# A two-layer diffusion step on one core: the low parts of layer 0's projection weights move from GpSimd to VectorE

## The chip, the core and the metric

The kernel runs on one core of one Trainium2 chip. The metric is device time in microseconds, the median of several runs. TensorE (PE) multiplies matrices, VectorE (DVE), ScalarE (ACT) and GpSimd (POOL) compute elementwise, and SyncE (SP) and GpSimd issue the DMAs. Each engine works through its own queue of instructions in the order in which the program lists them.

## The reference, cut to what matters

One inference step of a backbone with two layers, width 1024, for 512 latent tokens and 128 context tokens, in float32. Layer 0 projects the modulated input once, and splits the product between neighbourhood attention and RWKV-7 heads:

```python
proj = h @ w_in                                    # 1024 -> 3*512 + 1792
qa, ka, va, u = jnp.split(proj, [D_NA, 2 * D_NA, 3 * D_NA], axis=-1)
...
o_na = na_latent(qa, ka, va, na_ctx[0], na_ctx[1], rpb)   # softmax_attn_blocked for context tokens
o_rw, S_fin = rwkv_mixer(u, S0, *rw)                      # two directions, state scans
y = jnp.concatenate([o_na, o_rw], axis=-1) @ w_out
```

Then come a gated channel mixer (SwiGLU), layer 1 with differential attention and its mixer, and a final norm.

## The kernel before

Activations lie transposed: 128 features on the partitions, 640 tokens along the free dimension (512 latent, 128 context), in two halves of 320. Every large product is made of three: a float32 weight w is split into a rounded high part wh and the rest wl = w - wh, the input likewise into hh and hl, and TensorE adds wh x hh, wh x hl and wl x hh. `load_w` (L336) fetches a weight tile and splits it:

```python
        SY.dma_start(raw[:, 0:n], src)                                        # wr, L341
        ...
        A.copy(wh[:, 0:n], raw[:, 0:n])                                       # wh on ScalarE, L344
        eng = (V, G)[lo_turn[0] % 2] if cur.get("alt") else cur["lo"]         # L345
        lo_turn[0] += 1
        eng.tensor_tensor(wl[:, 0:n], raw[:, 0:n], wh[:, 0:n], ALU.subtract)  # wl, L347
```

Layer 0 has 26 projections of 128 output columns; each takes two such tiles of 128 x 512 (raw tiles: 3 buffers; wh and wl: 3 each) and 48 matmuls into PSUM tiles named `pj` (in the profile, all matmuls have line L99, that of the helper). The first four are computed ahead; `proj_units` (L1037) lists the rest: a gate, then for head pairs 1 to 3 the RWKV inputs k, r and v (`kkrv_proj`: ScalarE copies us, L966 to L971; VectorE shifts tokens, L973 and L975, and normalises, L251 to L262 and L996), then 12 tiles of the attention's q, k and v (`qk_proj`, written to DRAM as dn by GpSimd's DMA queue, L1031).

Four head pairs p go through the RWKV part one after the other. `prep(p)` (L1097) forms decays and keys (th L1119, at, kt, BX, KR), the score tiles psc (L1165), whose masked halves are Am and Bm (L1169, L1170), and then inverts 32 x 32 triangles: the score blocks go through DRAM (scr, L1173) into `mi` (L1178), 30 pairs of VectorE instructions (mt L1186, mi L1187) work on them, each on the result of the last, and mi goes back through DRAM (scr, L1190). Below this is called loop p. `mid(p)` (L1193) transposes (pbt), forms pax (L1237), fetches the inverse as MT (L1243), and composes the 64 x 64 inverse from c<-mi and c<-MT products. `chain(p)` (L1272) is the scan: 10 steps over 64 tokens, with VectorE, ScalarE, PE and GpSimd (sc, L1308) in turn. `gn(p)` (L1338) norms and gates and writes do[4 + p] (L1377).

`dense_b` (L1388) is the neighbourhood attention of the four pairs: it loads a mask (nam, L1390) and q, k and v back from dn (nqk, L1416, on SP's queue), forms scores (sna), softmax rows (L1397 to L1402), products (po) and writes do[p] (L1477); between them stand further adaLN products (pa). It uses the memory that the projections' input and weight tiles give free, so its first loads wait for the last pj. After scans and attention, `load_o` (L1577) fetches do, and the output projection begins.

The order on each engine is made by a scheduler when the program is built: it goes through the instructions by a priority number (low first among those that its own estimates of time hold ready). `prio` sets that number. The projections' loads, splits and copies have 100000 and so go ahead of `prep` and `chain`, which have 1000000 and more; the projections' matmuls alone have 5000000, and fill TensorE's queue where nothing else is ready:

```python
        prio(100000)
        cur["lo"] = G                      # L1502
        fill[0] = 5000000
        run(proj_units())
        low, fill[0] = fill[0], None
        cur["lo"] = V                      # L1506
        prio(base(0) - 50000)
        nxt = prep(0)
```

Elsewhere cur["lo"] is V: the four projections computed ahead, and all later stages.

Of the kernel before, what the change touches and what calls it, by code (L numbers as in the profile page):

```python
# [90 lines left out]
def tile_backbone(ctx: ExitStack, tc: tile.TileContext, I, O, stop=99):  # L91
    nc = tc.nc
    V, A, G, SY = nc.vector, nc.scalar, nc.gpsimd, nc.sync
# [38 lines left out]
    cur = {"lo": V}  # L132
# [742 lines left out]
    def prio(n):  # L875
        tc.cur_priority = n
# [5 lines left out]
    if True:  # L882
# [616 lines left out]
            return 1000000 + 100000 * p  # L1499

        prio(100000)
        cur["lo"] = G  # L1502
        fill[0] = 5000000
        run(proj_units())
        low, fill[0] = fill[0], None
# [600 lines left out]
```

## Time and profile before

| what | value |
|---|---|
| median of 3 runs | 2045.99 us (2042.53 to 2050.24) |
| profiled execution | 2047.56 us, span 2045.8 us |
| mean granted TensorE clock | 0.977 |
| busy share of the span | PE 95%, DVE 66%, ACT 39%, POOL 22% |
| low parts on POOL, whole program (L347) | 50, 72.2 us, mean 1448 ns |
| low parts on DVE, whole program (L347) | 124, 130.4 us, mean 1054 ns (most are twice as large) |
| loop 0, 1, 2, 3 (first mt to write-back) | 147 to 190, 246 to 286, 382 to 411, 511 to 546 us |
| attention's first loads, its last write | 426 and 651 us |
| last scan output written | 644 us |

A busy engine is one with an instruction in work; the ends of matmuls are modelled. A row of a group gives its line, engine, operation, output<-inputs, shapes and count, then the busy time in us and the mean of one in ns, then the idle time of the engine just before them and what ended it. A row of the timeline gives start, duration, engine, line and operands.

### The profile page before, as it was taken

What the parts mean: (1) busy time and instruction counts of PE and PEld (TensorE: products, weight loads), DVE (VectorE), ACT (ScalarE), POOL (GpSimd) and SP (SyncE); (2) the same over time, 40 slices, a digit from 0 to 9 for tenths busy, and PEclk for the clock granted to TensorE, in tenths of its full rate; (3) what the DMA queues carried; (4) which work ended last, traced back from release to release, by engine and by line L of the source; (5) the groups of instructions that cost most, each with busy time, mean ns of one, the idle gap of its engine ahead of it and who ended that gap; (6) DMA issues with size and microseconds to landing.
All of it is one profiled execution on the core that took longest, in us unless ns stands there. A gap on an engine that the chain in (4) does not pass through costs nothing.

```text
span 2045.8 us, 36390 instructions
## 1 busy us (share of the span) xinstructions
PE 1933.3 (95%) x14572; PEld 1720.3 (84%) x14572; DVE 1353.2 (66%) x2695; ACT 800.1 (39%) x1585; POOL 443.8 (22%) x451
## 2 busy tenths in 40 slices
PE   6888999978999999999999999999998899999998
PEld 2777787845466899999999988989988899999997
DVE  6559657656667697733772386788787866666665
ACT  3434342322445332212222255556554544343341
POOL 1233443433130210000000034233312311111100
PEclk8999999987999999999999999999999999999998
DMA  7433233262725255432442232111012132232222
GB/s 262 146 94 104 72 100 108 82 195 87 231 68 180 97 186 175 167 112 83 157 152 68 85 105 69 51 39 58 29 42 72 56 99 73 73 93 73 83 83 75
DMA packets 106129, 214.21 MB, mean 105 GB/s; under 512 B 33384, under 2 KB 43624, under 8 KB 102632
## 3 DMA queue, kind: packets, MB, share of 16 engines
q1 hardware_dynamic: 99080, 172.31, 27.1%
q0 software_dynamic: 6880, 39.59, 5.4%
q8 instruction: 114, 1.87, 0.4%
q14 instruction: 55, 0.45, 0.1%
HBM read 190.36 MB, written 23.44 MB: 105 GB/s over the span
## 4 chain that ended last, share of the span: by engine, by line
PE 63%; DVE 11%; DMA 4%; ACT 3%; issue 2%; POOL 1%; SPq 0%; ACTq 0%; DVEq 0%; POOLq 0%
PE ps L99 33%; PE pp L99 16%; PE c L99 2%; PE be L99 2%; PE sd L99 2%; DMA wr<-in_w 2%; PE psc L99 1%; PE y L99 1%; PE pj L99 1%; PE sna L99 1%; PE pa L99 1%; DVE mt L1186 1%; DVE wl L647 1%; PE po L99 1%; DVE mi L1187 1%
## 5 line engine op out<-in xcount | busy, mean ns | idle before, releaser
L344 ACT CAST wh<-wr 128x1024 fp32r<-128x1024 f32 (+3 forms) x174 | 143.1, 824 | 426.4 <-issue 189.0
L347 DVE TENSOR_TENSOR wl<-wr,wh 128x1024 fp32r<-128x1024 f32 (+2 forms) x124 | 130.4, 1054 | 130.5 <-ACT wh L344 129.6
L99 PE MATMUL ps<-hh,wh 128*128 128x320 f32 x592 | 185.7, 314 | 0.0
L99 PE MATMUL ps<-hl,wh 128*128 128x320 f32 x592 | 185.4, 313 | 0.2
L99 PE MATMUL ps<-hh,wl 128*128 128x320 f32 x592 | 185.2, 313 | 0.0
L99 PE MATMUL pj<-hh,wh 128*128 128x320 f32 x416 | 135.9, 328 | 7.6 <-ACT wh L344 5.0
L99 PE MATMUL ps<-bh,wh 128*128 128x320 f32 x432 | 134.9, 312 | 7.8 <-ACT top L757 6.4
L99 PE MATMUL pj<-hl,wh 128*128 128x320 f32 x416 | 137.5, 331 | 0.3 <-POOL hl L308 0.2
L99 PE MATMUL pj<-hh,wl 128*128 128x320 f32 x416 | 135.8, 327 | 1.5 <-POOL wl L347 1.5
L99 PE MATMUL ps<-bh,wl 128*128 128x320 f32 x432 | 134.1, 310 | 0.0
L99 PE MATMUL ps<-bl,wh 128*128 128x320 f32 x432 | 134.0, 310 | 0.0
L216 DVE SCALAR_TENSOR_TENSOR av<-wa,cs,av 128x512 f32<-128x512 f32 x182 | 123.9, 746 | 0.0
L347 POOL TENSOR_TENSOR wl<-wr,wh 128x512 fp32r<-128x512 f32 (+1 forms) x50 | 72.2, 1448 | 204.9 <-ACT wh L344 187.7
L99 PE MATMUL pp<-hh,wh 128*128 128x320 f32 x368 | 115.5, 314 | 0.0
L99 PE MATMUL pp<-hh,wl 128*128 128x320 f32 x368 | 114.0, 310 | 0.0
L99 PE MATMUL pp<-hl,wh 128*128 128x320 f32 x368 | 113.8, 310 | 0.0
L99 PEld LDWEIGHTS ps<-hh,wh 128*128 128x128 f32 x592 | 111.6, 189 | 2.2 <-ACT hh L465 0.8
L99 PEld LDWEIGHTS ps<-hl,wh 128*128 128x128 f32 x592 | 111.6, 188 | 2.1 <-issue 0.8
L99 PEld LDWEIGHTS ps<-hh,wl 128*128 128x128 f32 x592 | 111.6, 189 | 1.7 <-issue 1.5
L646 ACT CAST wh<-wr 128x1024 fp32r<-128x1024 f32 (+1 forms) x71 | 72.0, 1014 | 101.8 <-PE ps L99 61.0
L647 DVE TENSOR_TENSOR wl<-wr,wh 128x1024 fp32r<-128x1024 f32 (+1 forms) x71 | 88.8, 1251 | 16.0 <-ACT wh L646 15.8
L383 DVE SCALAR_TENSOR_TENSOR x<-ps,ada,x 128x192 f32<-128x192 f32 (+2 forms) x156 | 63.5, 433 | 50.2 <-PE ps L99 50.0
(409 smaller groups left out, 5625.9 us busy)
## 6 DMA issues: line engine op xcount, KB each, us to landing
wr<-in_w SPq DMA_DIRECT2D x88, 512.0 KB, 3.6
wa<-in_w_ada POOLq DMA_DIRECT2D x26, 1024.0 KB, 5.2
wa<-in_w_ada SPq DMA_DIRECT2D x88, 256.0 KB, 5.0
wr<-in_w_qk SPq DMA_DIRECT2D x16, 512.0 KB, 3.5
wr<-in_w2s SPq DMA_DIRECT2D x16, 512.0 KB, 3.6
wr<-in_w SPq DMA_DIRECT2D x19, 384.0 KB, 3.2
wr<-in_w_in_u SPq DMA_DIRECT2D x28, 256.0 KB, 2.9
wr<-in_w_in_qk SPq DMA_DIRECT2D x24, 256.0 KB, 2.9
```

The costliest lines, as they stand in the source:

```text
L99: i = nc.tensor.matmul(*a, **k)
L216: V.scalar_tensor_tensor(out=acc[s], in0=w[:, j], scalar=c, in1=acc[s], op0=ALU.mult, op1=ALU.add)
L344: A.copy(wh[:, 0:n], raw[:, 0:n])
L347: eng.tensor_tensor(wl[:, 0:n], raw[:, 0:n], wh[:, 0:n], ALU.subtract)
L383: V.scalar_tensor_tensor(out=xk[:, a:b], in0=pp[h][:, a - HT * h:b - HT * h], scalar=gate[:, m, s:s + 1], in1=xk[:, a:b], op0=ALU.mult, op ...
L646: A.copy(h, src)
L647: V.tensor_tensor(l_, src, h, ALU.subtract)
L1186: V.tensor_tensor(t3, bc(mi[:, rows, jj], 2, w), bc(mi[:, jj, cols], 1, jj), ALU.mult)
L1187: V.tensor_tensor(mi[:, rows, cols], mi[:, rows, cols], t3, ALU.add)
```

## The change

One line: the 44 low parts (two for each of 22 projections, 128 x 512 each) that `load_w` computes while `proj_units` runs go to VectorE. Nothing else in the code differs, but the scheduler, which reckons with other times, lists the instructions of every engine anew up to the output projection.

```diff
         prio(100000)
-        cur["lo"] = G
+        cur["lo"] = V
         fill[0] = 5000000
         run(proj_units())
         low, fill[0] = fill[0], None
         cur["lo"] = V
```

The names below end in a number that tells the buffers apart. The first place is VectorE's queue in the middle of loop 0 (mi_2589), with the projections' rows between. Before:

```order
L1186 TENSOR_TENSOR mt_2591<-mi_2589 80x240
L996 SCALAR_TENSOR_TENSOR ksq_995<-k_922,small,pkk_1164 128x320
L1187 TENSOR_TENSOR mi_2589<-mi_2589,mt_2591 80x16x15
L1186 TENSOR_TENSOR mt_2591<-mi_2589 80x240
L996 SCALAR_TENSOR_TENSOR ksq_995<-k_922,small,pkk_1167 128x320
L1187 TENSOR_TENSOR mi_2589<-mi_2589,mt_2591 80x15x16
L1186 TENSOR_TENSOR mt_2591<-mi_2589 80x238
```

Now:

```order
L1186 TENSOR_TENSOR mt_2591<-mi_2589 80x240
L347 TENSOR_TENSOR wl_1250<-wr_1247,wh_1249 128x512
L1187 TENSOR_TENSOR mi_2589<-mi_2589,mt_2591 80x16x15
L1186 TENSOR_TENSOR mt_2591<-mi_2589 80x240
L973 SCALAR_TENSOR_TENSOR rv_1091<-us_1104,small,rv_1091 128x511
L973 SCALAR_TENSOR_TENSOR rv_1091<-us_1104,small,rv_1091 128x127
L975 SCALAR_TENSOR_TENSOR rv_1091<-us_1104,small,rv_1091 128x511
L975 SCALAR_TENSOR_TENSOR rv_1091<-us_1104,small,rv_1091 128x127
L1187 TENSOR_TENSOR mi_2589<-mi_2589,mt_2591 80x15x16
L1186 TENSOR_TENSOR mt_2591<-mi_2589 80x238
```

A low part stands inside the loop now, and the shift of the next projection (rv_1091) has moved ahead by three pairs of the loop; in all the loop holds 10 low parts, and 127 instructions from its first to its end where it held 104.

The second place is TensorE's queue where mid(2) begins (c is its PSUM tile, pj_2349 and pj_2375 are the last two halves of a projection, pvt the transposes of the attention's first v). Before:

```order
L99 MATMUL pj_2349<-hh_358,wh_2345 128x320
L99 MATMUL c_5590<-mi_5585,Am_4997 32x32
L99 MATMUL c_5613<-mi_5585,Am_4997 32x32
L99 MATMUL pj_2349<-hl_359,wh_2345 128x320
L99 MATMUL pj_2349<-hh_358,wl_2346 128x320
```

Now:

```order
L99 MATMUL pj_2375<-hh_358,wh_2345 128x320
L99 MATMUL pj_2375<-hl_359,wh_2345 128x320
L99 MATMUL pj_2375<-hh_358,wl_2346 128x320
L106 MATMUL pvt_2903<-cst,nqk_2898 128x128 x4
L106 MATMUL pvt_2909<-cst,nqk_2898 128x128
L99 MATMUL c_5590<-mi_5585,Am_4997 32x32
L99 MATMUL c_5613<-mi_5585,Am_4997 32x32
```

Before, 29 matmuls of the last projection stand behind mid(2)'s first; now all stand ahead of it, and so do the attention's first transposes. Counted from the start, 562 pj stand ahead of mid(0)'s first c before and 659 now, 820 and 893 ahead of mid(1)'s, 1219 and 1248 (all) ahead of mid(2)'s.

The third place is SP's queue of DMAs at the same point: loop 2's way back (scr_5168, then MT), and the attention's first loads. Before:

```order
L341 DMA wr_2343<-in_w_in_qk 128x512
L1190 DMA scr_5168<-mi_5104 80x1024
L1243 DMA MT_5503<-scr_5168 32x20x32 x4
L1390 DMA nam<-in_na_mask 128x896
L1416 DMA nqk_2896<-dn 128x640
L1416 DMA nqk_2897<-dn 128x640
L1416 DMA nqk_2898<-dn 128x640
```

Now:

```order
L1178 DMA mi_5104<-scr_4926 80x1024
L1390 DMA nam<-in_na_mask 128x896
L1416 DMA nqk_2896<-dn 128x640
L1190 DMA scr_5168<-mi_5104 80x1024
L1416 DMA nqk_2897<-dn 128x640
L1416 DMA nqk_2898<-dn 128x640
L1243 DMA MT_5503<-scr_5168 32x20x32 x4
```

The mask and the first nqk load now stand ahead of loop 2's write-back, and the other two ahead of MT.

## The prediction

> **What bounds the kernel now.** I read the page first, then the stage that the change touches in stretches, then the chain of waits at its end, then VectorE's and GpSimd's rows in order of time. The page and GpSimd's largest group between 80 and 426 us:
>
> ```profile
> PE 1933.3 (95%) x14572; PEld 1720.3 (84%) x14572; DVE 1353.2 (66%) x2695; ACT 800.1 (39%) x1585; POOL 443.8 (22%) x451
> L347 POOL TENSOR_TENSOR wl<-wr,wh 128x512 fp32r<-128x512 f32 x44 | 62.8, 1432 | 99.1 <-ACT wh L344 85.7 <-PE pj L99 5.0 <-PE pvt L106 5.0
> ```
>
> The 44 rows that move take 62.8 us of GpSimd, and GpSimd stood idle 85.7 us ahead of them until ScalarE had the high part (wh) ready. TensorE is the busiest engine over the whole span, but the stage has other limits. Its stretches, cut at the ends of the inverse loops (mi, L1186/L1187); the columns are length, then busy time of PE, PEld, DVE, ACT and POOL, granted clock, DMA share, GB/s:
>
> ```profile
> 80.00:115.00 35.00, 25.55 (x140) 20.71 (x140) 24.84 (x31) 16.70 (x30) 16.86 (x18) 0.90 0.45 148
> 115.00:147.00 32.00, 30.70 (x252) 23.59 (x252) 8.89 (x28) 13.07 (x29) 9.10 (x8) 0.89 0.34 96
> 147.00:191.00 44.00, 38.57 (x225) 32.22 (x225) 42.89 (x109) 17.79 (x33) 17.32 (x15) 0.95 0.30 104
> 191.00:212.00 21.00, 20.16 (x269) 17.47 (x269) 18.30 (x29) 10.07 (x20) 9.97 (x9) 0.93 0.39 94
> 212.00:246.00 34.00, 33.51 (x349) 24.57 (x347) 16.32 (x53) 8.01 (x20) 12.08 (x16) 1.00 0.26 72
> 246.00:287.00 41.00, 40.01 (x391) 32.90 (x391) 35.96 (x100) 17.76 (x41) 18.32 (x21) 1.00 0.29 93
> 287.00:303.00 16.00, 15.70 (x243) 13.95 (x239) 1.67 (x2) 6.22 (x15) 4.89 (x5) 1.00 0.44 117
> 303.00:382.00 79.00, 77.94 (x690) 58.30 (x689) 48.24 (x111) 26.12 (x61) 31.69 (x41) 1.00 0.31 95
> 382.00:410.00 28.00, 28.00 (x251) 27.14 (x250) 26.08 (x59) 9.22 (x20) 12.12 (x12) 1.00 0.24 78
> 426.00:500.00 74.00, 58.90 (x486) 34.18 (x484) 48.22 (x111) 18.44 (x45) 27.53 (x38) 0.82 0.46 148
> ```
>
> Read the DVE column: in the inverse loops of pairs 0, 1 and 2 (147 to 191, 246 to 287, 382 to 410) VectorE is busy 42.89 of 44, 35.96 of 41 and 26.08 of 28 us. There it sets the pace. Between the loops it has air, and PE is nearly full. So added VectorE time costs in the loops and little between them. The chain of waits at the stage's end:
>
> ```profile
> 410.63 3.20 DMA scr<-mi
> 413.90 2.09 DMA MT<-scr
> 417.00 0.41 PE c L99 x4
> 417.42 6.50 PE pj L99 x27
> 423.92 1.38 PE c L99 x76
> 425.29 0.50 PE pj L99 x2
> 427.02 7.40 DMA nqk<-dn
> ```
>
> The path runs from the end of loop 2 through two DMAs to mid(2)'s first products (c), then through 27 leftover projection matmuls (pj), and after the last pj to the loads (nqk) with which the attention heads start.
>
> **The added and the removed rows.** What a low part costs on VectorE stands in the first 80 us, where eight are computed there already:
>
> ```profile
> L347 DVE TENSOR_TENSOR wl<-wr,wh x8: 682/690/692, 27.9 to 67.3; 128x512 fp32r<-128x512 f32 x8
> ```
>
> 44 x 0.690 = 30.4 us are added to VectorE. Against it stands what GpSimd's rows do to VectorE now. GpSimd and VectorE in the same 5 us of loop 2:
>
> ```profile
> 387.65 1.51 POOL L347 TENSOR_TENSOR wl<-wr,wh 128x512 fp32r<-128x512 f32 x1 [11.13 <-ACT wh L344]
> 389.41 1.30 POOL L347 TENSOR_TENSOR wl<-wr,wh 128x512 fp32r<-128x512 f32 x1 [0.24 <-ACT wh L344]
> ...
> 387.23 0.36 DVE L1187 TENSOR_TENSOR mi<-mi,mt 80x198 f32<-80x198 f32 x1
> 388.04 1.36 DVE L1187 TENSOR_TENSOR mi<-mi,mt 80x210 f32<-80x210 f32 x1
> 389.43 1.52 DVE L1186 TENSOR_TENSOR mt<-mi 80x220 f32<-80x220 f32 x1
> 390.98 0.38 DVE L1187 TENSOR_TENSOR mi<-mi,mt 80x220 f32<-80x220 f32 x1
> ```
>
> A row of 0.36 to 0.38 us lasts 1.36 or 1.52 when a GpSimd low part runs beside it. I went through all 44 and compared each VectorE row that overlaps one with the shortest of its form: 30 rows are longer by 0.09 to 2.67 us, 28.0 us in all. The first and the last, each with its usual length beside it:
>
> ```profile
> 94.55 1.66 DVE L1134 TENSOR_SCALAR bs<-kt,small 128x640 f32<-128x640 f32 x1
> L1134 DVE TENSOR_SCALAR bs<-kt,small x4: 539/548/1659, 94.5 to 455.1; 128x640 f32<-128x640 f32 x4
> ...
> 382.60 0.22 DVE L1187 TENSOR_TENSOR mi<-mi,mt 80x58 f32<-80x58 f32 x1
> 408.96 1.20 DVE L1187 TENSOR_TENSOR mi<-mi,mt 80x58 f32<-80x58 f32 x1
> ```
>
> By stretch they are 4.6 us before 147, 7.1 in loop 0, 2.5 at 206 to 211, 4.7 in loop 1, 2.0 between 303 and 382, and 7.1 in loop 2. So VectorE's net load is 30.4 - 28.0 = +2.4 us. The Trainium skill, SBUF — State Buffer, section "Who interferes with whom", has it that an instruction of VectorE with two SBUF inputs and one of GpSimd that reads SBUF exclude each other for the whole instruction; by that rule a low part of 1.43 us could cost up to 44 x 1.43 = 63 us, and the rows show less than half, because many meet no such row.
>
> **Where it falls.** The two built orders say where the 44 rows stand now. Three go ahead of prep(0)'s first row, where VectorE has idle time, six between there and loop 0, 10 in loop 0, 4 behind it up to mid(0)'s second transpose, 2 up to loop 1, 4 in loop 1, 4 behind it, 8 up to loop 2 and 3 in it. The projections' other VectorE rows moved along with them; their prices from loop 0:
>
> ```profile
> L973 DVE SCALAR_TENSOR_TENSOR k<-us,small,k 128x511 f32<-128x511 f32 (+1 forms) x2 | 1.0, 536 | 0.0
> L996 DVE SCALAR_TENSOR_TENSOR ksq<-k,small,pkk 128x320 f32<-128x320 f32 x2 | 1.1, 540 | 0.1
> L259 DVE SCALAR_TENSOR_TENSOR rt<-rt,rm 128x160 f32<-128x160 f32 x5 | 1.6, 314 | 0.0
> ```
>
> - Before loop 0: six rows, 4.1 us, against 4.6 of relief: 0.
> - Loop 0: 10 low parts (6.9), and drawn forward from later 8 shift rows (L973, and L975 priced as L973; 8 x 0.54 = 4.3), two of L996 (1.1) and small ones (2.1): +14.4. Relief 7.1. The loop is full, so +7.3.
> - To mid(0)'s transpose: 4 low parts and small rows, +4.1; 2.7 of 21 us are idle. I take +3.0 (0 to 4.1).
> - To loop 1: +1.3 against 2.5, half idle: 0.
> - Loop 1: 4 low parts (2.8) less the rows that left (8.9): -6.1; relief 4.7 makes -10.8. VectorE is busy 88% there, so I take -9.5 (-10.8 to -6.1).
> - 287 to 303: 2.8 us under 14 idle ones: 0.
> - To loop 2: +5.5 less 2.0, at 61% busy; I take half, +1.7 (0 to 3.5).
>
> Loop 2 so starts later by 7.3 + 3.0 - 9.5 + 1.7 = 2.5 us (-3.5 to +8.8). In loop 2 it is 3 x 0.69 - 7.1 = -5.0.
>
> Here the order pays. In the order before, 206 projection matmuls stand behind prep(2)'s last products (pax); now 121. The price of one, from the pj rows alone in loop 2:
>
> ```profile
> 382.00:410.00 28.00, 24.71 (x167) 24.22 (x166) 2.61 (x7) 1.00 0.24 78
> ```
>
> 24.71 / 167 = 0.148 us, so 85 fewer are 12.6 us: the last pj ends 2.5 - 12.6, about 10 us earlier, and the attention loads with it. Mid(2) gains less: on SP's queue the write-back of loop 2 (scr<-mi) now stands behind the first nqk load, which waits for the last pj. Loop 2 ends 2.5 us earlier, pj near 416 us, so the write-back leaves some 5 us later than 410.6; the 27 pj (6.50 us) no longer stand between the c's. Net about -1.5 to -3.5.
>
> What is at the end decides how much of it stays:
>
> ```profile
> L1377 SPq DMA_DIRECT2D do<-ysq x4: 319/320/326, 320.8 to 644.4; - x4
> L1477 SPq DMA_DIRECT2D do<-nqk x4: 320/326/384, 546.3 to 651.4; - x4
> ```
>
> The attention heads write last, 7.0 us behind the scans. Attention 10 us earlier and scans 2.5 earlier leave the end at 641.4 against 641.9: at most -9.5. The two share VectorE and PE, and only 15.1 of the 74 us from 426 to 500 are idle on PE, so I take two thirds, -6.5 (-9.5 to 0). GpSimd's queue loses its 44 waits; its DMA issues and the state scaling (sc) leave sooner, priced 0, since VectorE and PE rows release them.
>
> **The wait that is added.** A low part on VectorE waits for wh, and the rows behind it in VectorE's queue wait too. ScalarE's own wait ahead of wh:
>
> ```profile
> ACT wh L344 <- PE pj L99: 48.5, 29, 4.8
> ```
>
> In the loops VectorE is the late one and finds wh ready. Outside them stand 27 low parts; at GpSimd's mean wait of 85.7 / 44 = 1.95 us that is at most 53 us, at least 0. VectorE's idle time there is 10.2 + 23.1 + 17.7 + 14.3 + 30.8 = 96 us, so I take +1.5, near the lower end. Sum: -6.5 + 1.5 = -5.0. The profiled execution took 2047.56 us (span 2045.8), 0.1% over the median 2045.99; **2047.6 - 5.0, about 2042 us**. That is within the 0.5% (10.2 us) that a measurement of this kernel can tell from no change.
>
> **Rivals.**
> - *VectorE's queue becomes the wait* (slower). If the 14 low parts between the loops 0 and 2 that lie outside a full loop (2, 4 and 8) each cost their 1.95 us of waiting on the path, 27.3 us replace the 1.5: 2047.6 - 6.5 + 27.3 = 2068. For it: VectorE runs in order, and the long waits of ScalarE ahead of wh. Against it: the idle time there. It decides from 16.7 us of waiting on the path. Chance 0.22.
> - *The relief does not come*, because the lengthened rows were waiting for something else. Then loop 0 costs 14.4, loop 1 -5.4, the stretch to loop 2 2.7, and loop 2 starts 14.7 us later and lasts 2.1 longer; the last pj ends 14.7 - 12.6 = 2 us later, the scans, without the 6.5 of pj, 10.3. They would write last at 654.7, 3.3 us later than now: with the 1.5 of waiting 2052. Against it: 30 rows lengthened beside a low part, equal shapes next to them not. Chance 0.08. The Trainium skill, Perfetto Trace Analysis, "Optimizing Scalar/DVE Operations", speaks for this rival in one half: a saturated VectorE may give work away, even to GpSimd. Its other half, that between these two it might not help since they share a read port, is what the lengthened rows agree with.
> - *All of it arrives* (faster). Every term at its lower end: loop 2 starts 3.5 earlier, the last pj ends 3.5 + 12.6 = 16 us earlier, and the scans follow: 2047.6 - 16 = 2031. Against it: the scans' 7 us. Chance 0.25.
>
> **How the numbers follow.** The forecast has 0.45, with its own range 2034 to 2051 (the sums at -9.5 - 4 and at 0 + 3.5). Faster by over 0.5% (under 2035.8): 0.25 and a sliver of the forecast, 0.28. Slower (over 2056.2): 0.22 and the upper edges of the forecast and of the second rival, 0.26. Within: 0.46. With about a tenth left out at each side, the range runs from below the fast rival to just short of the slow one, 2026 to 2066.
>
> **What would show it.** Right: no loop row of VectorE of 1.3 us or more, loop 0 about 50 us long, loop 1 about 31, loop 2 about 23; the last pj before 420 us and nqk loads before it was 426; mid(2)'s c rows in one piece. Wrong: VectorE idle ahead of wl for wh by over 15 us in 200 to 380, or the loops as long as now, or the scans' last write later than 644 us by itself.

## The result, and the profile after

The changed kernel took 2054.89 us (median of 8 runs, 2053.05 to 2062.88), the kernel before 2044.79 beside it (8 runs): ratio 1.0061, interval 1.0046 to 1.0075. So it is slower by about 0.6%, some 10 us to 13 us, where 2042 was forecast. The profiled execution of the changed kernel took 2054.58 us (span 2052.5), 7.0 us more than that of the kernel before (2047.56): the traces can account for 7 of the 10 to 13 us. Two executions far from the rest, one of the kernel before (2130.47 us) and one of e8 (5021.17 us), are left out of the ratios here and below.

The page of the changed kernel, engine totals and the low parts on VectorE:

```profile
PE 1943.3 (95%) x14572; PEld 1726.2 (84%) x14572; DVE 1352.0 (66%) x2739; ACT 797.9 (39%) x1585; POOL 390.5 (19%) x407
L347 DVE TENSOR_TENSOR wl<-wr,wh 128x1024 fp32r<-128x1024 f32 (+3 forms) x168 | 160.7, 958 | 158.7 <-ACT wh L344 155.5
```

VectorE has 44 instructions more and is busy no longer than before (1352.0 against 1353.2): the low parts it took over cost what GpSimd's had cost it. The three loops, each from its first row to its end (columns as before):

```profile
139.00:191.00 52.00, 50.08 (x357) 43.54 (x353) 50.51 (x137) 24.40 (x46) 10.33 (x11) 1.00 0.37 125
244.00:283.00 39.00, 36.89 (x308) 29.80 (x307) 28.78 (x88) 12.86 (x32) 8.97 (x17) 0.96 0.24 77
384.00:408.00 24.00, 21.32 (x198) 20.39 (x194) 21.38 (x64) 5.76 (x12) 3.82 (x12) 1.00 0.16 54
```

Loop 0 is longer, loops 1 and 2 are shorter, as forecast. Where it then goes wrong is seen from the starts of a few instructions (us, from the two traces):

| place | before | after | difference |
|---|---|---|---|
| loop 0: first row, write-back | 147.3, 190.4 | 139.4, 190.3 | -7.9, -0.1 |
| loop 1: first row, write-back | 246.4, 286.5 | 244.7, 282.3 | -1.7, -4.2 |
| loop 2: first row, write-back | 381.9, 410.6 | 384.0, 408.0 | +2.1, -2.6 |
| mid(2)'s last copy (MT, L1269) | 428.2 | 421.8 | -6.4 |
| prep(3)'s first load (k, L1100) | 436.2 | 438.9 | +2.7 |
| prep(3)'s first mask (Am, L1169) | 469.7 | 474.0 | +4.3 |
| scans' last write (do, L1377) | 644.4 | 646.7 | +2.3 |
| attention's last write (do, L1477) | 651.4 | 648.6 | -2.8 |
| output projection's second part, first load (L1553) | 667.1 | 671.1 | +4.0 |
| layer 1's output projection, first load (L1553) | 1543.1 | 1549.7 | +6.6 |

Up to mid(2) the change gains 6.4 us. From mid(2)'s last copy to prep(3)'s first mask it took 41.4 us before and 52.3 now: there the gain is lost, and 4.3 more. The chain of waits of the changed kernel in this stretch (start, length, what):

```profile
408.01 4.13 DMA scr<-mi
...
413.13 2.68 DMA MT<-scr
415.83 0.85 DVE mi L1253
416.73 5.91 PE c L99 x158
422.64 1.58 PE sna L99 x4
424.22 1.36 PE c L99 x2
425.58 1.58 PE sna L99 x4
...
442.87 0.42 PE sna L99 x2
443.29 0.97 PE pa L99 x2
444.26 1.27 PE c L99 x4
```

The c rows of mid(2) come in one piece, as forecast. But behind them the path runs over TensorE's rows of the attention: scores (sna), adaLN products (pa), transposes and outputs, until at 444.26 (its place on the chain; 444.19 on TensorE's timeline) the product c<-r of gn(1) gets its turn, behind which prep(3)'s first products stand. It was at 440.83 before. The row before, then after:

```profile
440.83 1.34 PE L99 MATMUL c<-r,cst 128*128 128x320 f32 x4
```

```profile
444.19 1.34 PE L99 MATMUL c<-r,cst 128*128 128x320 f32 x4
```

That is 12.6 us behind mid(2)'s last copy before and 22.4 now. VectorE tells the same of the rows that make this r (L253 to L262). Its timeline before, first and last of them:

```profile
431.39 0.33 DVE L253 TENSOR_SCALAR rm<-y 128x160 f32<-128x160 f32 x1 [1.37 <-PE y L99]
434.91 0.32 DVE L260 SCALAR_TENSOR_TENSOR rs<-rt,rs 128x160 f32<-128x160 f32 x1
438.58 0.82 DVE L262 TENSOR_TENSOR r<-rs,cst 128x640 f32<-128x640 f32 x1
```

And after:

```profile
429.62 0.33 DVE L253 TENSOR_SCALAR rm<-y 128x160 f32<-128x160 f32 x1 [1.63 <-PE pa L99]
434.06 0.69 DVE L1397 CUSTOM_DVE_ANT_0 s<-sna,bm 128x512 f32<-128x512 f32 x1 [2.55 <-PE sna L99]
436.20 0.69 DVE L1397 CUSTOM_DVE_ANT_0 s<-sna,bm 128x512 f32<-128x512 f32 x1 [1.21 <-PE sna L99]
439.57 0.32 DVE L260 SCALAR_TENSOR_TENSOR rs<-rt,rs 128x160 f32<-128x160 f32 x1
439.92 0.82 DVE L262 TENSOR_TENSOR r<-rs,cst 128x640 f32<-128x640 f32 x1
```

From rm to the last rs it was 3.8 us, all in one run; now it is 10.3, since softmax rows that wait for TensorE's sna stand between. The first places in the queue went to the attention. The last pj now ends at 405.3 and not at 425.8, so the attention's rows can be ready earlier; that the scheduler, which orders by its own estimates when the program is built, listed them earlier for this reason fits, but its estimates are not on record.

The scans win back 2.0 us of the 4.3 by their last write, and the table hides a second loss. At loop 3's first row they had won back all of it (510.7 before, 510.6 now), but loop 3 then lasts 38.0 us instead of 35.0. VectorE waits longer in it for the scan's product c. Its waits for c ahead of S, before and then after:

```profile
DVE S L1310 <- PE c L99: 0.6, 2, 0.3
```

```profile
DVE S L1310 <- PE c L99: 3.1, 2, 2.5
```

The other 4.3 of the final 6.6 are lost behind the scans, 1.7 of it where the output projection begins. Its first product on TensorE's timeline, before and then after:

```profile
651.40 0.38 PE L99 MATMUL ps<-sh,wh 128*128 128x320 f32 x1 [0.31 <-ACT nqk L1474]
```

```profile
653.71 0.60 PE L99 MATMUL ps<-sh,wh 128*128 128x320 f32 x1 [5.46 <-DMA wr<-in_w_out]
```

It comes 7.0 us behind the scans' last write in both (and 6.4 to 7.4 us behind it in every run below, while the attention's last write varies from 1.5 us ahead of the scans' to 7.1 us behind it). But before, the attention still kept TensorE busy until then; now the attention has ended, TensorE stands idle for 5.46 us, and the first 120 products are slower. The stretch from 650 to 660 us before (columns as above, the granted clock third from the end) and after, and the products on the chain of waits, before and after:

```profile
650.00:660.00 10.00, 9.43 (x64) 8.97 (x64) 9.09 (x17) 6.70 (x12) 0.00 (x0) 1.00 0.81 257
```

```profile
650.00:660.00 10.00, 6.29 (x31) 6.32 (x32) 7.47 (x12) 6.34 (x10) 0.00 (x0) 0.66 0.88 277
```

```profile
651.41 17.84 PE ps L99 x120
```

```profile
653.72 19.59 PE ps L99 x120
```

The last 2.6 us, up to layer 1, stay unexplained.

### The profile page after: what moved, and what is told of

Its sections match the earlier page's. It is cut to its first block, busy times and chain, and to the rows that moved or that the text cites. A ratio compares the mean times of both kernels' runs of the same rounds, so it can differ in the third digit from the quotient of the medians.

```text
span 2052.5 us, 36389 instructions
## 1 busy us (share of the span) xinstructions
PE 1943.3 (95%) x14572; PEld 1726.2 (84%) x14572; DVE 1352.0 (66%) x2739; ACT 797.9 (39%) x1585; POOL 390.5 (19%) x407
## 3 DMA queue, kind: packets, MB, share of 16 engines
q1 hardware_dynamic: 99080, 172.31, 26.7%
## 4 chain that ended last, share of the span: by engine, by line
PE 75%; DVE 10%; DMA 5%; ACT 4%; issue 3%; POOL 2%; SPq 0%; DVEq 0%; ACTq 0%; POOLq 0%
PE ps L99 33%; PE pp L99 16%; PE pj L99 6%; PE c L99 3%; PE psc L99 2%; PE y L99 2%; PE be L99 2%; PE sna L99 2%; PE sd L99 2%; PE pa L99 2%; DMA wr<-in_w 1%; PE po L99 1%; DVE wl L347 1%; PE pt L106 1%; PE pw L99 1%
## 5 line engine op out<-in xcount | busy, mean ns | idle before, releaser
L344 ACT CAST wh<-wr 128x1024 fp32r<-128x1024 f32 (+3 forms) x174 | 143.1, 823 | 421.8 <-issue 173.9
L347 DVE TENSOR_TENSOR wl<-wr,wh 128x1024 fp32r<-128x1024 f32 (+3 forms) x168 | 160.7, 958 | 158.7 <-ACT wh L344 155.5
L647 DVE TENSOR_TENSOR wl<-wr,wh 128x1024 fp32r<-128x1024 f32 (+1 forms) x71 | 88.8, 1251 | 16.7 <-ACT wh L646 15.1
L99 PEld LDWEIGHTS pj<-hh,wh 128*128 128x128 f32 x416 | 80.9, 195 | 13.7 <-ACT wh L344 5.4
## 6 DMA issues: line engine op xcount, KB each, us to landing
wr<-in_w SPq DMA_DIRECT2D x19, 384.0 KB, 3.1
```

Of the source, the lines that this page charges most:

```text
L99: i = nc.tensor.matmul(*a, **k)
L647: V.tensor_tensor(l_, src, h, ALU.subtract)
```

## The experiments

Theory 1: moving the rows is a gain by itself, and the new order of all engines' queues loses it. Theory 2: the 44 rows on VectorE and its waits for wh cost the time. To tell them apart, the order and the engine of the low parts were set apart. A kernel can be made to issue in a recorded order, by an ordering edge (no wait) between each instruction and the one ahead of it on its engine in the record:

```diff
+    pin(tc, ORDER)                      # end of tile_backbone; ORDER: the instructions of a build, in its order
...
+        if i.engine in last:
+            tc.add_manual_dep(i, last[i.engine].name, edge, reason="recorded order")
+        last[i.engine] = i
```

No run shows the old record on the kernel before alone. That the edges themselves cost little is seen from e11, which has the changed kernel's order as a record and only some loads moved: its loop 0 lasts 50.9 us, as in the changed kernel, and mid(2)'s last copy to prep(3)'s first mask 52.0 instead of 52.3. A record can also be cut: one order up to some instruction, another from there on. "Old" is the order of the kernel before, "new" that of the changed one. All ratios are to the kernel before, run beside it.

**e1: old order, low parts on VectorE.** The changed kernel with the old record.

> The 44 low parts stand on VectorE, but every engine issues in the order that the kernel before was built with (the low parts stand in VectorE's queue where the common order has them). Theory 1, the re-made order loses what the move gains: without it the move is neutral or a small gain, because 28.0 us of lengthened VectorE rows go and 30.4 us of low parts come, and in loop 2 three low parts (2.1 us) replace 7.1: ratio 0.997 to 1.000 (2039 to 2045 us beside 2045), loop 2 about 5 us shorter than 28.7. Theory 2, the added rows and VectorE's wait for the high parts cost the time: the loss stays without any new order, ratio 1.004 to 1.008 (2053 to 2061).

**e2: new order, low parts on GpSimd.** The kernel before with the new record.

> The 44 low parts are back on GpSimd, but every engine issues in the order that the changed kernel was built with. Theory 1, the re-made order loses: the loss stays, and the lengthened rows come on top (28.0 us on VectorE, of which the loops show 7.1, 4.7 and 7.1 before): ratio 1.005 to 1.009 (2055 to 2063 us). Theory 2, VectorE's added rows lose: the loss goes with them, ratio 0.998 to 1.002.

| ratio (interval) | low parts on GpSimd | low parts on VectorE |
|---|---|---|
| old order | 1 (2044.58) | e1: 0.9959 (0.9944 to 0.9975), 2039.30 |
| new order | e2: 1.0130 (1.0103 to 1.0157), 2072.56 | 1.0061 (1.0046 to 1.0075), 2054.89 |

The move gains in either order, 0.4% and 0.7%; the new order loses about 1% with either engine. Theory 2 is out. The last writes of scans and attention in e1:

```profile
L1377 SPq DMA_DIRECT2D do<-ysq x4: 319/320/327, 317.3 to 637.0; - x4
L1477 SPq DMA_DIRECT2D do<-nqk x4: 319/330/384, 538.7 to 644.0; - x4
```

Both are 7.4 us earlier than before (644.4, 651.4), and mid(2)'s last copy 7.6: in the old order nothing of the gain is lost behind mid(2). Loop 2 lasts 27.3 us there, not the 23 or 24 that I expected, and loop 0 40.2 instead of 43.1: the gain comes from more places than loop 2. In time the gain is 0.41%, 8.4 us, with an uncertainty of about 3.

**e3 and e4: a cut at the last pj.** Low parts on VectorE; e3 new then old, e4 old then new.

> Low parts on VectorE; the order of the changed kernel up to the last projection matmul (near 404 us in its trace), from there on the order of the kernel before. Theory 1 in its narrow form, the order behind the projections loses: the 6.4 us that stood at mid(2)'s matrices are kept, and the write of the scans comes about 6 us before 644.4: 2037 to 2042 us, ratio 0.996 to 0.9985. Theory 2: as the changed kernel, 1.004 to 1.008.

> Low parts on VectorE; the order of the kernel before up to the last projection matmul (near 425 us in its trace), from there on that of the changed kernel. Theory 1 in its narrow form: the loss is made behind the projections, ratio 1.003 to 1.007 (2051 to 2059 us). If the loss came from the order of the projections themselves: ratio 0.997 to 1.000. Theory 2: 1.004 to 1.008, and then the run above shows it too.

e4 measured 1.0056 (1.0038 to 1.0074), 2057.77: the order behind the projections loses it all. Its last scan write:

```profile
L1377 SPq DMA_DIRECT2D do<-ysq x4: 319/320/326, 314.6 to 654.1; - x4
```

It is 17.1 us later than in e1, which has the same queues up to the last pj. Of these, 7.3 stand already at mid(2)'s last copy (427.9 against 420.6): on e4's chain of waits the attention's first transposes (pvt), with 6.59 us for their nqk load, come ahead of mid(2)'s last 42 c. From there to the first mask it is 51.5 against 41.0. e3 measured 1.0004 (0.9980 to 1.0027), which fits neither theory, and its 12 runs fall into two groups: five at 2035.6 to 2040.5 us with a mean clock of 0.979 to 0.981, seven at 2049.6 to 2055.0 with 0.970 to 0.975. The profiled run is of the slower group. TensorE's timeline in it, and its stretches from 314 us on:

```profile
318.35 0.44 PE L99 MATMUL c<-S,KR 128*64 128x128 f32 x4 [2.71 <-DVE vT L1368]
```

```profile
314.00:316.00 2.00, 1.65 (x11) 1.30 (x9) 0.00 (x0) 0.85 (x2) 0.00 (x0) 1.00 0.90 328
316.00:318.00 2.00, 0.00 (x0) 0.00 (x0) 0.19 (x1) 0.00 (x0) 0.00 (x0) 1.00 1.01 396
318.00:320.00 2.00, 1.65 (x16) 1.14 (x16) 1.93 (x5) 0.44 (x2) 0.00 (x0) 1.00 0.27 106
320.00:322.00 2.00, 2.00 (x14) 0.94 (x12) 1.34 (x3) 0.77 (x2) 0.91 (x1) 0.56 0.02 6
...
334.00:336.00 2.00, 2.00 (x17) 1.55 (x17) 1.26 (x4) 1.52 (x3) 0.19 (x1) 0.50 0.00 0
336.00:338.00 2.00, 2.00 (x16) 1.57 (x17) 0.80 (x3) 0.00 (x0) 0.93 (x2) 0.68 0.38 131
338.00:340.00 2.00, 2.00 (x35) 1.63 (x35) 1.27 (x4) 0.63 (x2) 0.00 (x0) 1.00 0.00 0
```

TensorE waits 2.71 us for vT (whose load took 6.9 us to land, behind a weight load), and then runs at half clock (column PEclk) for 17 us, busy all the time. In the profiled run of the changed kernel the same instruction waited 0.78 us and the clock stayed at 1.00. The Trainium skill, TensorE: Matmul & The Clock Gate, section "Part 1: The HAM clock gate", has it that an idle window of about 3.4 us can halve the clock and that one busy window of that length brings it back; the first agrees only roughly (2.71 us sufficed), the second not: here the return took 17 us of full TensorE, and the measurement decides. Elsewhere in the same trace the return was quick: behind a wait of 2.72 us that ended at 278.7 the clock was 0.82, 0.50 and 0.83 in three windows of 2 us and 1.00 from 284 on. What makes the difference stays open.

**e5: e3 with two loads moved.** On SyncE's queue vT and gt (L1366, L1372) go ahead of one weight load.

> The order of e3 (new up to the last projection matmul, then old; low parts on VectorE), and on SyncE's queue alone two loads of the first normalization (vT, gt; L1366, L1372) stand ahead of one projection weight load instead of behind it. In e3 the runs fell into two groups, five at 2036 to 2041 us with a mean clock of 0.979 to 0.981 and seven at 2050 to 2055 with 0.970 to 0.975; its profiled run, of the slower group, shows TensorE idle for 2.71 us at 315.6 for that vT, and then 17 us at a granted clock of 0.50. Theory C (the clock: a gap of TensorE costs more than its length, and the new order makes such gaps): vT comes about 1.5 us earlier, the gap falls under 1.5 us, and most runs are of the faster group: median 2035 to 2041, ratio 0.995 to 0.998. Theory S (SyncE's queue and VectorE set the time, the clock only follows): no change, median 2050, ratio 0.998 to 1.003.

It measured 0.9965 (0.9954 to 0.9976), 2040.89, and the slow group is gone (2035.7 to 2046.2 in 12 runs). In its trace this product does not wait and the clock stays at 1.00. From it to loop 2's first row it takes 69.4 us, and 75.7 in e3; the rest of the 13 us between the groups lies further on. So the new order up to the last pj costs nothing that can be measured but that gap, and with the old order behind it the move is the gain that e1 shows. The same long half clock stands in the profiled runs of e2, e6 and e8, behind waits of 2.00, 2.13 and 1.65 us of the same product for vT, and so is part of their times; the changed kernel's (0.78) and e13's (1.57) do not have it.

**e6: new order, TensorE's gap filled.** Behind the last pj TensorE was idle for 8.60 us and the clock 0.50 thereafter.

```diff
                 pm = cps("c", 2)
+                for _ in range(36 if p == 2 and h == 0 else 0):
+                    PE.matmul(pm.rearrange("p (a b) -> p a b", a=4), lhsT=warm, rhs=bc(warm[:, :], 1, 4), start=True, stop=True)
```

> The changed kernel in its own order, with 36 matmuls of no use (lhsT=warm) in TensorE's queue right behind the last projection matmul, where TensorE stood idle for 8.60 us (405.3 to 413.9) and the granted clock was 0.50 from 410 to 430. Theory C: the clock stays near 1.00 to 430, mid(2)'s 160 small products take about 3 us instead of 5.9 and what follows up to 430 gains as much: 4 to 8 us, 2047 to 2051, ratio 1.001 to 1.003. Theory S: prep(3)'s loads still leave at 439 behind 15 adaLN weight loads, and the time stays at 2053 to 2057, ratio 1.004 to 1.007.

It measured 1.0056 (1.0035 to 1.0077): no gain beyond the uncertainty. Its stretches:

```profile
410.00:420.00 10.00, 10.00 (x60) 9.23 (x59) 7.68 (x26) 0.85 (x2) 2.81 (x11) 1.00 0.44 140
420.00:430.00 10.00, 7.88 (x127) 6.55 (x127) 1.67 (x2) 2.06 (x6) 1.46 (x2) 0.84 0.87 248
430.00:440.00 10.00, 10.00 (x93) 5.70 (x90) 2.64 (x8) 4.18 (x10) 6.82 (x9) 0.50 0.42 141
```

The filling held the clock while it lasted, and the half clock came ten microseconds later. From loop 2's write-back to prep(3)'s first mask it took 65.2 us, and 66.0 in the changed kernel. As the half clock was only moved, the run does not show what this stretch takes without it. That the clock alone is not the cause is shown by e5 above and e11 below: between mid(2)'s last copy and the first mask the mean granted clock was 0.84 in e5 and 0.86 in e11, and the time 40.6 and 52.0 us.

**e7: old order, the 44 low parts left out.** The third product then takes wh, and the results are not those of the kernel.

```diff
+        if eng is None:                                  # while proj_units runs
+            G.memset(wl[:, 0:1].bitcast(F32), 0.0)
+            tc.cur_priority = at
+            return (wh[:, 0:n].rearrange("p (k c) -> p k c", k=kn),) * 2
...
-        cur["lo"] = V
+        cur["lo"] = None
```

> The order of the kernel before, and the 44 low parts left out: the third product takes the high part (wh), and a one-column memset on GpSimd stands in the low part's place. It prices the 44 rows on VectorE against e1 (2039.3), and the relief against the kernel before. If the rows cost the path what they last in the loops (6.9, 2.8 and 2.1 us), it is 8 to 12 us under e1: 2027 to 2031, ratio 0.991 to 0.994. If VectorE takes them in its idle time: 2035 to 2039, ratio 0.995 to 0.998. If the relief were nothing and e1's gain came from elsewhere: as before, 1.000.

It measured 0.9888 (0.9868 to 0.9907). Engine totals of its page:

```profile
PE 1927.0 (95%) x14572; PEld 1716.1 (85%) x14572; DVE 1325.0 (65%) x2695; ACT 799.4 (39%) x1585; POOL 384.5 (19%) x451
```

With the same instructions as before, VectorE is busy 1353.2 - 1325.0 = 28.2 us less: that is what GpSimd's low parts did to it. Leaving them out gains 1.1%, 23 us of the path, in which the waits of GpSimd's queue and of TensorE for wl are included. On VectorE the rows and their waits for wh give back 0.9959 - 0.9888 = 0.7%, about 14.5 us, with an uncertainty of about 5, where the rows last 30.4. Expected were 8 to 12 if the loops alone made the cost: 14.5 is above that, though not beyond the uncertainty. The loops show 11.3 of it (40.2, 39.9 and 27.3 us in e1, 36.7, 37.6 and 21.7 here). About half of the rows is hidden by VectorE's idle time.

**e8: one ordering edge for the scheduler, no record.**

```diff
+                if p == 2:
+                    tc.add_manual_dep(adal[36].ins, prepl[11].ins.name, NOSYNC, reason="scan first")
```

> The changed kernel, no recorded order, and one ordering edge for the scheduler: the fifth adaLN weight load of the attention stage (wa) is issued behind prep(3)'s last load (r). The scheduler makes the order anew around it. Theory S: gn(1)'s and prep(3)'s loads leave near 428 instead of 437 to 446, the scans write last near 638 to 641 instead of 646.7, 2043 to 2049, ratio 0.999 to 1.002. Theory C: the gap at 405 to 414 and the half clock behind it stay, and the gain is under 3 us: 2051 to 2056, ratio 1.003 to 1.006.

It measured 1.0068 (1.0046 to 1.0090). The loads left 9.4 us behind mid(2) instead of 17.1, and the first mask came 49.8 behind it: the scheduler put other attention rows there, 32 sna where the changed kernel has 24. The time is above both expected ranges.

**e9 and e10: which part of the order.** Three pieces: up to the last pj, from there to prep(3)'s last load, and the rest. e9 is new, new, old; e10 new, old, new; loads as in e5, which is new, old, old.

> Low parts on VectorE, loads vT and gt moved as in e5. The order is the changed kernel's up to prep(3)'s last load (445.6 us in its trace), and from there on that of the kernel before; e5 has the new order only up to the last projection matmul (405 us). Theory S1, the 41 us in between lose the time (15 adaLN weight loads ahead of gn(1)'s and prep(3)'s loads, attention rows ahead of theirs): ratio 1.001 to 1.004, as e5 plus 9 to 14 us. Theory S2, the loss is made behind it, where the scans and the attention share the engines to 650 us: as e5, 0.995 to 0.998.

> The counterpart: the changed kernel's order up to the last projection matmul, that of the kernel before from there to prep(3)'s last load, and the changed kernel's again behind it (vT and gt as in e5). Theory S1: the loss is gone but for the late weight loads of the output projection (1.7 us) and what the joint costs: 0.996 to 0.999. Theory S2: the loss stays, 1.002 to 1.006.

e9 measured 1.0005 (0.9993 to 1.0018), just below the range of S1: the 41 us in the middle cost 0.4% against e5, 8 us with an uncertainty of about 3.5. The scans write last at 642.3, 8.4 us later than in e5. e10, which should have been without it, measured 1.0099 (1.0081 to 1.0117), the opposite of what S1 gives: with the new order behind the old piece, prep(3)'s loads do leave early (426.4), but the attention rows that the new order has ahead of this point now all come behind the loads and in front of prep(3)'s products, and the first mask stands 61.2 us behind mid(2). So e10 does not answer the question of S1 or S2; it says that the place of these rows costs, not which record they are from.

**e11: new order, three loads moved.** vT, gt and the first two weight loads of the output projection.

> The changed kernel's own order, but on SyncE's queue vT and gt as in e5, and the first two weight loads of the output projection (wr from w_out) ahead of the last writes of the attention and the scans, where the kernel before has them. In the changed kernel the first weight load left at 648.95 and the first product came 7 us behind the scans' last write at 646.7; in the kernel before the weights were there. If these loads make what is lost behind 645 us: 2 to 4 us less than the changed kernel, and no run of a second, slower group: ratio 1.002 to 1.004. If the start waits for the outputs (o) alone: as the changed kernel, 1.005 to 1.006.

It measured 1.0033 (1.0021 to 1.0046). But the output projection starts no sooner: its first product is at 652.95, 6.9 us behind the scans' last write, after 5.32 us of waiting, now for ScalarE's wh. I had read that wait as one for the weights; the 7 us behind the scans are the same in the kernel before. Of the 0.28% gained, 0.19% either way, I can name only the gap at vT, and the profiled run of the changed kernel does not show a half clock behind it; so the gain has no shown cause. Against e5, which has the old order behind the last pj, e11 is 0.68%, 13.9 us, slower: its scans write last 12.1 us later (646.0 against 633.9), 11.9 of it by the first mask.

**e12 and e13: adaLN weight loads on GpSimd's queue.**

```diff
-            SY.dma_start(w, I["w_ada"][l, n, :, k, :])
+            eng.dma_start(w, I["w_ada"][l, n, :, k, :])     # G in the attention stage
```

> The changed kernel's own order on every engine (vT and gt as in e5), but the attention stage's 56 adaLN weight loads (wa) are issued by GpSimd instead of SyncE, each at its place in the common order. In the changed kernel 15 of them stood ahead of gn(1)'s and prep(3)'s loads on SyncE and were issued from 415.9 to 437.4, 9.7 us of it waiting for a buffer that TensorE had to free. From the last row of mid(2) to the first product mask of prep(3) (Am) it took 52.2 us there, 41.5 in the kernel before, and between 40.6 and 42.8 in every run with the old order at this place. Theory S1 in its sharp form, SyncE's queue holds prep(3): its loads leave within 9 us of mid(2) instead of 17, Am comes 42 to 45 us behind mid(2), and the time falls by 7 to 10 us: 2042 to 2046, ratio 0.998 to 1.001. Rival, the queues of TensorE and VectorE hold it (attention rows stand ahead of prep(3)'s there too): the loads leave early, Am still comes 50 us or more behind mid(2), 2051 to 2055, ratio 1.003 to 1.005.

> The changed kernel with the 56 adaLN weight loads on GpSimd's queue and no recorded order: the scheduler plans anew with SyncE free of them. If SyncE's queue is what holds the scans, and the scheduler does not give it back elsewhere: 2038 to 2046, ratio 0.996 to 1.001. If a plan made anew again puts attention rows ahead of prep(3)'s, as with the one edge of e8: 2050 to 2062, ratio 1.003 to 1.008.

e12 measured 1.0063 (1.0044 to 1.0083), e13 1.0137 (1.0112 to 1.0162), both above the ranges expected: a plan made anew was worse again. In e12 mid(2)'s last copy, prep(3)'s first load (SyncE), c<-r (TensorE) and the first mask (VectorE) stand so:

```profile
424.77 0.84 ACT L1269 COPY MT<-c 32x320 f32<-32x320 f32 x2 [0.22 <-PE c L99]
...
428.47 0.42 SPq L1100 DMA_DIRECT2D k<-du  x1
...
447.71 1.34 PE L99 MATMUL c<-r,cst 128*128 128x320 f32 x4
...
478.18 0.42 DVE L1169 TENSOR_TENSOR Am<-psc,cst 128x256 f32<-128x256 f32 x1
```

The load leaves 3.3 us behind mid(2)'s last copy and not 17, and the mask still comes 53 us behind it; c<-r stands 22.5 us behind it, as in the changed kernel (22.4). SyncE's queue is not what holds prep(3). Of the other queues, those of TensorE and VectorE have attention rows on the way to c<-r; ScalarE's and GpSimd's were not tested by themselves. TensorE's adaLN products in the stretch, before and after (columns PE, PEld, DVE, ACT, clock, DMA):

```profile
428.00:469.00 41.00, 6.01 (x16) 0.88 (x16) 0.00 (x0) 0.58 (x1) 0.89 0.70 236
```

```profile
422.00:474.00 52.00, 13.91 (x32) 2.21 (x32) 0.00 (x0) 1.17 (x2) 0.83 0.51 170
```

With sna, transposes (pt) and outputs (po) it is 9.7 us of attention rows before and 26.6 after. Every kernel without shortened rows falls on one of two sides:

| kernel | attention rows on TensorE in the stretch, us | mid(2)'s last copy to first mask, us |
|---|---|---|
| before, e1, e3, e5, e7 | 9.7, 9.9, 11.9, 10.7, 9.6 | 41.4, 41.0, 42.9, 40.6, 41.4 |
| after, e2, e4, e6, e11, e12 | 26.6, 25.5, 25.5, 25.8, 26.3, 25.6 | 52.3, 51.5, 51.5, 51.6, 52.0, 53.0 |
| e8, e9, e10, e13 | 26.7, 23.1, 25.7, 21.1 | 49.8, 50.2, 61.2, 49.7 |

Loop 3 divides the same kernels but for e9, which has the old order again by then: 34.5 to 35.0 us with the old order there (e9 34.7), 38.0 to 48.6 with another.

**e14 and e15: some of these rows made short.** In e11's order (e14) and in e5's (e15). The adaLN values are then incomplete.

```diff
-    def ada_mm(wts, pa):
+    def ada_mm(wts, pa, part=512):
...
-            PE.matmul(pa[32 * g:32 * g + 32, :], lhsT=cs[:, k, :], rhs=w, start=hi == 0, stop=hi == 1,
+            n = part if hi else 512
+            PE.matmul(pa[32 * g:32 * g + 32, 0:n], lhsT=cs[:, k, :], rhs=w[:, 0:n], start=hi == 0, stop=hi == 1,
...
-        ada_mm(ada_load(l, n, tp), pa)
+        ada_mm(ada_load(l, n, tp), pa, 4)       # in the attention stage
```

> The order of e11 (the changed kernel's), and of the attention stage's 56 adaLN products (pa, 128x512) every second half is cut from 512 columns to 4: 28 rows of TensorE shrink, 16 of them between mid(2)'s last row and prep(3)'s Am, about 7 us at the 0.43 us that one takes there; adaLN values are so wrong, the loads stay. Theory, the attention rows in TensorE's queue hold prep(3): the stretch from mid(2) to Am falls from 52 us to 45 to 47, the scans write last 5 to 7 us earlier than in e11 (646.0), and the ratio is 0.999 to 1.001 instead of 1.0033. Rival, prep(3) waits for loads or VectorE's own rows, and the attention rows only fill TensorE's waiting: the stretch stays at 50 or more, ratio 1.002 to 1.004.

> The same cut in e5, where the old order stands behind the projections and only 16 adaLN products lie in that stretch, 8 of them cut (3 us). Theory: the stretch falls by 0 to 3 us from 40.6, and the whole by less than in the run before: ratio 0.994 to 0.9965, 0.9965 without the cut. Rival: both fall alike.

e14 measured 0.9986 (0.9974 to 0.9999), 0.47% or 9.6 us less than e11; e15 0.9948 (0.9936 to 0.9959), 0.17% or 3.5 us less than e5. The same 28 short rows are worth nearly three times as much in the new order, though the uncertainty is wide: about 3.6 us on the 9.6 and 3.3 on the 3.5. The stretch itself shrank by only 2.5 us in e14 (52.0 to 49.4), not by 5 to 7, though the adaLN rows there fell from 13.6 to 8.0 us: the clock from 430 to 440 was 0.50 and not 0.82. In e15 it even grew, from 40.6 to 44.3, at a mean clock of 0.69 and not 0.84. Of the 8.3 us by which the scans write earlier in e14 than in e11 (637.8, 646.0), 4.4 come in loop 3 (38.1 to 33.7 us), where VectorE's wait for c falls from 3.1 us to 1.2. That attention rows in TensorE's queue cost the scans time is so borne out, for loop 3 better than for the stretch ahead of it. That they lengthen the stretch rests on its chain of waits and on the table; how its 11 us divide between TensorE's rows, VectorE's r in pieces and the clock stays open.

## Why the prediction was wrong

| step | predicted | measured |
|---|---|---|
| VectorE's net load | +2.4 us (30.4 - 28.0) | -1.2 (page); relief 28.2 (e7) |
| loop 0 | +7.3 | 43.1 to 50.9: +7.8 |
| to mid(0)'s end | +3.0 | +2.5 (MT copy 210.9 to 213.3, write-back the same) |
| to loop 1 | 0 | 35.5 to 31.4: -4.1 |
| loop 1 | -9.5 | 40.1 to 37.6: -2.5 |
| to loop 2 | +1.7 | 95.4 to 101.7: +6.3 |
| start of loop 2 | +2.5 | +2.1 |
| loop 2 | -5.0 | 28.7 to 24.0: -4.7 |
| last pj | -10 | 425.8 to 405.3: -20 |
| mid(2)'s last copy | -1.5 to -3.5 | -6.4 (the write-back left at 408.0, not near 416) |
| end of the stage | -6.5 | scans +2.3, attention -2.8 |

- Right: the mechanism. GpSimd's low parts lengthen VectorE's rows by 28 us, the loops are where that counts, and moving the rows gains. No loop row of 1.3 us or more is left. With the old order e1 shows -7.4 us at both last writes; that this is near the -6.5 taken is chance, since the -6.5 came from the new order (85 fewer pj in the way), which e1 does not have. The rival that the relief does not come (2052) is refuted by e7, though its number is near the time measured.
- Right, but by luck: the start of loop 2. The gain in loop 1 was over-sized by 7.0 us and the cost of the stretch behind it under-sized by 4.6, and against that loop 0 started 7.9 us earlier and the stretch from mid(0) to loop 1 took 4.1 us less, both of which I had at 0.
- Right: the added wait is small. VectorE stood idle ahead of wl for wh for 13.1 us between 200 and 380 us, under the 15 that I had set. The rival in which this wait decides (2068; its sum passes 2056.2 from 15.1 us of waiting, not 16.7) did not happen: e1 has such waits too (11.9 us), and gains. But the rows themselves are not free: e7 prices them, with their waits, at about 14.5 us of the path, less than the 23 that come back without GpSimd's.
- Wrong, and this is the step that failed: "what is at the end decides how much of it stays", where I took two thirds of 9.5 us. I let the attention come 10 us earlier and called that a gain, since it wrote last. It came 20 us earlier, and its rows went into the queues of TensorE and VectorE ahead of gn(1) and prep(3), on which the scans hang. I knew that "the two share VectorE and PE" and priced it as one third; it was all of the gain and more: 41.4 us became 52.3, and loop 3 35.0 became 38.0. Nor does the last write decide: the attention wrote last 2.8 us earlier than before, and the output projection still began 2.3 us later, 7.0 us behind the scans. My own sign for being wrong was the scans' last write later than 644, and it came at 646.7.
- Missing altogether: that a new order moves TensorE's gaps. At the output projection's start a gap of 5.46 us and the clock behind it (0.66) went with 1.7 us more for the first 120 products, and in e3 a load of vT that comes late goes with a slow group of runs, some 13 us above the other, that e5 does not have.

## What to carry to other kernels

When a change makes a list scheduler plan anew, price the new order at every place where two chains share an in-order queue, not only where the edit is: work of the less urgent chain can be listed earlier, ahead of rows on which the urgent chain waits. Set the two effects apart by putting the recorded order of the one build on the other; of this change the move alone was worth -0.4%, and the order +1.0%. The version to keep is the move with the old order (e1, 0.9959), or e5 (0.9965), both faster than either kernel.

## What the runs showed of the hardware

- A short gap of TensorE can be followed by a long stretch at half clock, and its length alone does not tell. At one place of this program, where the product c<-S,KR waits for vT, gaps of 1.65 (e8), 2.00 (e2), 2.13 (e6) and 2.71 us (e3) were followed by 17 to 24 us at a granted clock near 0.50, with TensorE busy; gaps of 0.78 (changed kernel) and 1.57 us (e13) by none. At another place in e3's trace a gap of 2.72 us was made good within 6 us. The gap of 8.60 us in the changed kernel (405 to 414) stood ahead of 0.50 from 410 to 430. What sets the length of the return was not tested.
- GpSimd's 44 low parts, 62.8 us, kept VectorE busy 28.2 us longer, as the rows read one by one had said (28.0). The Trainium skill, SBUF — State Buffer, "Who interferes with whom", lets an instruction of VectorE with two SBUF inputs and one of GpSimd that reads SBUF exclude each other; the total does not contradict it, as 28.2 is under the 62.8 that every low part would cost in full.
- 30.4 us of rows on an engine that is busy 66% of the span cost, with their waits, about 14.5 us of the path (e7 against e1, uncertainty about 5): about half is hidden.
